# Adaptive-norm modulation of two feed-forward stages: running sums on VectorE in place of matmuls on TensorE

## Chip, cores, metric

One Trainium2 chip; the kernel runs on one of its cores. The metric is the device time of one execution in microseconds. The engines are TensorE (PE; its weight loads are listed apart as PEld), VectorE (DVE), ScalarE (ACT), GpSimd (POOL) and SyncE (SP), whose queue issues the DMAs here.

## What is computed

Two layers of a hybrid backbone over 512 latent tokens and 256 context tokens, width 1024. Each layer is a half-step SwiGLU feed-forward, a mixer of four head groups, and a second half-step feed-forward. Each of the three parts is modulated by vectors that come from one conditioning vector per stream (`c` for the latent, `c_ctx` for the context tokens):

```
mod   = (silu(c)     @ w_mod[l] + b_mod[l]).reshape(BATCH, 9, 1, 1024)
mod_c = (silu(c_ctx) @ w_mod[l] + b_mod[l]).reshape(9, 1, 1024)
x  = x  + 0.5 * mod[:, 2] * swiglu(modulate(rms_norm(x,  norm_g[l, 0]), mod[:, 0], mod[:, 1]), ffn_w_in[l, 0], ffn_w_out[l, 0])
xc = xc + 0.5 * mod_c[2]  * swiglu(modulate(rms_norm(xc, norm_g[l, 0]), mod_c[0],  mod_c[1]),  ffn_w_in[l, 0], ffn_w_out[l, 0])
...
```

`w_mod[l]` is 1024 x 9216 in f32, 37.7 MB for each of two layers. It is read once, and only two vectors are multiplied by it. In the second layer the context stream needs no output, so the context's vectors 5 to 8 are not needed there.

## The kernel before

The feed-forwards run in the order (layer 0, i = 0), mixer, (0, 1), (1, 0), mixer, (1, 1); they are called the first to the fourth below. `ffn` splits the 2816 hidden columns into 22 steps of 128. For each step `up` (line 520 for its matmuls) makes seven products of 12 matmuls out of the loaded weights `w1r`: ScalarE takes the high part `w1h` (line 460), VectorE the low part `w1l` (line 461) and the sums and differences of weights (line 479), in four buffers each. VectorE then combines the products (lines 525, 568, 581, 586). After every chunk of 3 or 2 steps (`CK` is 3, 2, 2, 3, 3, 3, 3, 3) the down-projection follows: products `y` (lines 448, 450, 452) with `w2h` and `w2l`, which VectorE adds to the residual `xT` (line 615). In the program the products of a step are put in before the down-projection of the chunk ahead of it, so both interleave on TensorE.

Modulation runs in the background of the first three feed-forwards, in blocks of 512 columns: 14, 6 and 12 blocks, from the list `bg` in `build`. A block is loaded in two halves of 1 MB (`mod_load`, line 229, one buffer `wm`); per half `mod_some` issues four f32 matmuls (line 241). Each has the 32-column tile `sc` (the two vectors and zeros) as its weight and 512 columns of `w_mod` as moving data, and writes its own 32 rows of one PSUM bank. After the second half ScalarE copies the bank to `mrow` (line 210), four matmuls against `pick` (line 218) add up the four row groups and transpose them, and VectorE adds the result to `mod` (line 221).

What sets the order: the program is written with tiles, and the framework puts each engine's instructions into a fixed order when the program is built, by the order of issue in the program and by priorities. `high_priority(offset=-LATER)` with `LATER = 300` places what is inside it as if it had been issued 300 instructions later; `mod_load` and `mod_some` stand inside it. `mod_flush` is called at fixed places of `up` at normal priority. On the chip every engine, and SP's queue of DMA issues, takes its instructions strictly in that order. The last chunk of the second feed-forward reuses the buffers `pc`, `sg` and `wm` for nine held tiles (`held_open`).

Of the kernel before, what the change touches and what calls it, by code (L numbers as in the profile page):

```python
# [18 lines left out]
F32 = mybir.dt.float32  # L19
# [4 lines left out]
ALU = mybir.AluOpType  # L24
# [4 lines left out]
KT = 8  # L29
# [3 lines left out]
DEPTH = 2  # L33
DFF = 2816
# [37 lines left out]
def more_constants():  # L72
    f = np.float64
    r = np.arange(128)
    d = r % 64

    ax = np.zeros((128, 128)); sq = np.zeros((128, 128))
    for i in range(128):
        h = i % 32
        j = i + 16 if h < 16 else i - 16  # L80
        ax[j, i] = -1.0 if h < 16 else 1.0
        h = i % 64
        j = i + 32 if h < 32 else i - 32
        sq[j, i] = -1.0 if h < 32 else 1.0
    tok = np.arange(SEQ)
    inv16 = (1.0 / (np.float32(ROPE_BASE) ** (np.arange(0, 32, 2, dtype=np.float32) / np.float32(32)))).astype(np.float32)
    inv32 = (1.0 / (np.float32(ROPE_BASE) ** (np.arange(0, 64, 2, dtype=np.float32) / np.float32(64)))).astype(np.float32)
    pos = np.where(d[:, None] < 32, tok[None, :] // GRID_W, tok[None, :] % GRID_W).astype(np.float32)
    aa = (pos * inv16[d % 16][:, None]).astype(np.float32).astype(f)
    sa = (tok[None, :].astype(np.float32) * inv32[d % 32][:, None]).astype(np.float32).astype(f)  # L90

    lg = np.log1p(-np.exp2(-5.0 - np.arange(4)))
    i = np.arange(128)
    rel = i[None, :] - i[:, None]
    dm = np.zeros((128, 4, 2, 128))
    for h in range(4):
        dm[:, h, 0] = np.where(rel >= 0, np.exp(np.maximum(rel, 0) * lg[h]), 0) / 8
        dm[:, h, 1] = np.where(rel <= 0, np.exp(np.maximum(-rel, 0) * lg[h]), 0) / 8
    qs = np.zeros((128, 2, 2, 128)); ks = np.zeros((128, 2, 2, 2)); gc = np.zeros((128, 2))
    for j in range(2):  # L100
        for e in range(2):
            g = lg[2 * j + e]
            qs[64 * e:64 * e + 64, j, 0] = np.exp((i + 1) * g)[None, :]
            qs[64 * e:64 * e + 64, j, 1] = np.exp((128 - i) * g)[None, :]
            ks[:, j, 0, e] = np.exp((127 - i) * g) / 8
            ks[:, j, 1, e] = np.exp(i * g) / 8
            gc[64 * e:64 * e + 64, j] = np.exp(128 * g)
    mean64 = (r[:, None] // 64 == r[None, :] // 64) / 64.0
    comb = r[:, None] % 32 == np.arange(2)[None, :]

    mp = np.where(i[None, :] >= i[:, None], 0, NEG)
    mn = np.where(i[None, :] <= i[:, None], 0, NEG)
    c32 = lambda *xs: np.concatenate([x.reshape(128, -1) for x in xs], 1).astype(np.float32)
    return {"k_rope": c32(ax, sq, np.cos(aa), np.sin(aa), np.cos(sa), np.sin(sa), mean64),
            "k_ret": c32(dm, qs, ks, gc), "k_win": c32(mp, mn), "k_comb": c32(comb)}
# [6 lines left out]
class Whole:  # L122
# [90 lines left out]
    def mod_add(self, l, b, row):  # L213

        nc = self.nc
        pt = self.psum("modpt", "ms")
        for j in range(4):
            nc.tensor.matmul(pt[:, 2 * j:2 * j + 2], lhsT=row[:, j * 128:(j + 1) * 128], rhs=self.pick, start=True, stop=True)  # L218
        for v in range(2):
            m = self.mod[l][v][:, b:b + 4]  # L220
            nc.vector.tensor_tensor(out=m, in0=pt[:, v:8:2], in1=m, op=ALU.add)
# [25 lines left out]
    def mod_flush(self):  # L247
        if self.mod_row:
            self.mod_add(*self.mod_row)
            self.mod_row = None  # L250

    def scales(self, l, n, v):

# [294 lines left out]
    def ffn(self, l, i, segs, chunks, background, last_cb, switch):  # L548
        nc, a = self.nc, self.a
        w2 = a["ffn_w_out"]  # L550
        H = self.half
        self.mod_now = self.mod_row = None
        self.mod_todo = [(*t, h) for t in background for h in range(2)]
        f = 0
        for ci, cn in enumerate(chunks):
            gs = []
            for j in range(cn):
                ff = f + j
                first = l == i == ff == 0
                if ff == 0:  # L560
                    ahead = self.up(l, i, 0, first)
                    if first:
                        self.first_shifts()
                    else:
                        self.raw_rows(self.fw, segs)
                t, g, p = ahead
                n1 = 2 * H
                mul = lambda eng, out, x, y: eng.tensor_tensor(out=out, in0=x, in1=y, op=ALU.mult)  # L568
                mul(nc.vector, g[:, :H], p[:, 2:H + 2], self.rsb[:, :H])
                mul(nc.vector, g[:, H:], g[:, H:], self.rsb[:, H:])  # L570
                mul(nc.vector, t[:, 2:], t[:, 2:], self.rsb)
                if first:
                    b = self.bias0
                else:
                    b = self.fw.tile([128, 2, 2], F32, name="ub", tag="ub", bufs=2)
                    nc.scalar.copy(b[:, 0, :], t[:, 0:2])
                    nc.scalar.copy(b[:, 1, :], p[:, 0:2])
                for s, (o, n) in enumerate(segs):
                    nc.scalar.activation(out=g[:, o:o + n], in_=g[:, o:o + n], func=AF.Silu, bias=b[:, 1, s:s + 1])
                for s, (o, n) in enumerate(segs):  # L580
                    nc.vector.scalar_tensor_tensor(out=g[:, o:o + n], in0=t[:, 2 + o:2 + o + n], scalar=b[:, 0, s:s + 1], in1=g[:, o:o + n],
                                                   op0=ALU.add, op1=ALU.mult)
                gh = self.hl.tile([128, n1], F32R, name="gh", tag="gh", bufs=max(chunks))
                gl = self.hl.tile([128, n1], F32R, name="gl", tag="gl", bufs=max(chunks))
                nc.scalar.activation(out=gh[:, :n1], in_=g[:, :n1], func=AF.Copy)  # L585
                nc.vector.tensor_tensor(out=gl[:, :n1], in0=g[:, :n1], in1=gh[:, :n1], op=ALU.subtract)
                gs.append((gh, gl))
                with self.tc.high_priority(offset=-LATER):
                    if ff:
                        self.mod_some()  # L590
                    else:
                        self.mod_load()

                if ff < DFF // 128 - 1:
                    ahead = self.up(l, i, ff + 1, False)
                if j == cn - 2:
                    wo = self.raw.tile([128, cn, D], F32, name="wo", tag="wo", bufs=1)
                    for q in range(cn):
                        nc.sync.dma_start(out=wo[:, q, :], in_=w2[l, i, (f + q) * 128:(f + q + 1) * 128, :])
            self.mod_flush()  # L600
            if ci == 0:
                gt = self.gates(l, 2 * i, segs, 0.5)
            if ci == len(chunks) - 1:
                if switch:
                    switch()
                else:
                    self.held_open([(self.fw, "pc", NPC, 1), (self.fw, "sg", 1, 2), (self.raw, "wm", 1, 3)])
            for n_ in range(KT):
                wh, wl = self.split(wo[:, :, n_ * 128:(n_ + 1) * 128], [128, cn, 128], "w2")
                py = [self.psum("y", "u")[:, :n] for o, n in segs]  # L610
                for j in range(cn):
                    self.mm3(py, wh[:, j, :], wl[:, j, :], gs[j][0], gs[j][1], segs, j == 0, j == cn - 1)
                for s, (o, n) in enumerate(segs):
                    xs = self.xT[n_][:, o:o + n]
                    nc.vector.scalar_tensor_tensor(out=xs, in0=py[s], scalar=gt[s][:, n_:n_ + 1], in1=xs, op0=ALU.mult, op1=ALU.add)  # L615
                if ci == len(chunks) - 1:
                    if switch is None and last_cb == self.fin_tile:

                        if n_:
                            last_cb(n_ - 1)  # L620
                        if n_ == KT - 1:
                            last_cb(n_)
                    else:
                        last_cb(n_)
            f += cn
# [454 lines left out]
    def ffn_open(self, ctx):  # L1080
        self.raw = self.pool(ctx, "raw", 3)
        self.hl = self.pool(ctx, "hl", 2)
        self.fw = self.pool(ctx, "fw", 2)
        self.pick = self.fw.tile([128, 2], F32, name="pick", bufs=1)
        self.nc.sync.dma_start(out=self.pick, in_=self.a["k_comb"])

    def first_mods(self):

# [633 lines left out]
```

## Time and profile before

| | us |
|---|---|
| median of 3 runs | 3520.66 (3515.94 to 3521.97) |
| the profiled execution | 3524.8 |
| its span from first to last instruction | 3522.7 |

| engine | busy us | share of the span |
|---|---|---|
| TensorE matmul | 3323.0 | 94% |
| TensorE weight load | 2799.4 | 79% |
| VectorE | 2403.3 | 68% |
| ScalarE | 1536.0 | 44% |
| GpSimd | 163.6 | 5% |

Durations below come from the profiled execution. Busy time is the time in which at least one instruction of the engine runs; neighbouring instructions overlap a little, so the sum of durations can be larger. In the chain that ended last the products of the up-projection (line 520) hold 32% of the span, the `y` products 18%, the modulation's matmuls (line 241) 2% and their transposes (line 218) 1%.

### The profile page before, as it was taken

How to read it: one execution, taken by the hardware profiler on the slowest of the kernel's cores; microseconds unless marked ns; L12 is line 12 of the kernel's file. 1: busy time of each engine (PE TensorE's matmuls, PEld its weight loads, DVE VectorE, ACT ScalarE, POOL GpSimd, SP SyncE). 2: the span in 40 equal slices, each digit the busy share in tenths (PEclk: the TensorE clock that was granted, in tenths of full speed). 3: DMA queues.
4: the chain of work that ended last, by engine and by line, in shares of the span. 5: the costliest groups of instructions: out<-in, count | busy, mean ns of one | idle time of the engine just before them, and what ended most of it. 6: DMA issues, size and time to landing. Idle time of an engine off the chain costs nothing.

```text
span 3522.7 us, 58995 instructions
## 1 busy us (share of the span) xinstructions
PE 3323.0 (94%) x23204; PEld 2799.4 (79%) x23204; DVE 2403.3 (68%) x5252; ACT 1536.0 (44%) x3342; POOL 163.6 (5%) x342
## 2 busy tenths in 40 slices
PE   6999999999998997999999899999999989989998
PEld 3888889777775664998999788988788776658997
DVE  5667667555547776676677866666645567868887
ACT  4333333422447653443344533433433467644554
POOL 0000000000003220000000000000000012300000
PEclk8899999999999898999999899999999989999999
DMA  5333333211100002233321233333312100022332
GB/s 184 108 121 122 103 108 107 81 43 43 43 14 1 11 16 71 77 97 111 104 67 51 90 102 111 110 98 105 102 54 56 37 9 7 19 86 88 108 99 72
DMA packets 329861, 267.63 MB, mean 76 GB/s; under 512 B 30676, under 2 KB 278640, under 8 KB 329584
## 3 DMA queue, kind: packets, MB, share of 16 engines
q1 hardware_dynamic: 329584, 263.87, 24.1%
q8 instruction: 182, 2.98, 0.3%
q14 instruction: 95, 0.78, 0.1%
HBM read 261.72 MB, written 2.10 MB: 75 GB/s over the span
## 4 chain that ended last, share of the span: by engine, by line
PE 81%; DVE 12%; ACT 4%; DMA 2%; issue 1%; POOL 1%; SPq 0%; DVEq 0%; ACTq 0%; POOLq 0%
PE ul L520 32%; PE y L448 6%; PE y L452 6%; PE y L450 6%; PE pj L448 4%; PE pj L450 4%; PE pj L452 4%; PE op L1479 3%; PE modps L241 2%; PE S L1224 1%; PE ch L959 1%; PE modpt L218 1%; DVE xtmp L902 1%; PE po L1224 1%; PE gram L830 1%
## 5 line engine op out<-in xcount | busy, mean ns | idle before, releaser
L520 PE MATMUL ul<-bh,w1h 128*128 128x386 f32 (+3 forms) x2464 | 809.2, 329 | 17.0 <-ACT w1h L460 6.1
L520 PE MATMUL ul<-bl,w1h 128*128 128x386 f32 (+3 forms) x2464 | 804.6, 327 | 0.6 <-DVE bl L348 0.4
L520 PE MATMUL ul<-bh,w1l 128*128 128x386 f32 (+3 forms) x2464 | 801.8, 326 | 2.7 <-DVE w1l L461 2.6
L460 ACT ACTIVATE w1h<-w1r 128x512 fp32r<-128x512 f32 x528 | 328.8, 631 | 491.4 <-PE ul L520 441.0
L520 PEld LDWEIGHTS ul<-bh,w1h 128*128 128x128 f32 x2464 | 467.9, 190 | 50.5 <-issue 20.1
L461 DVE TENSOR_TENSOR w1l<-w1r,w1h 128x512 fp32r<-128x512 f32 x528 | 360.3, 689 | 193.1 <-ACT w1h L460 185.4
L520 PEld LDWEIGHTS ul<-bl,w1h 128*128 128x128 f32 x2464 | 469.0, 190 | 9.5 <-issue 4.2
L520 PEld LDWEIGHTS ul<-bh,w1l 128*128 128x128 f32 x2464 | 467.3, 190 | 6.7 <-DVE w1l L461 4.2
L615 DVE SCALAR_TENSOR_TENSOR xT<-y,gate,xT 128x512 f32<-128x512 f32 x448 | 267.3, 631 | 176.5 <-PE y L452 174.3
L448 PE MATMUL y<-gh,w2h 128*128 128x512 f32 x1232 | 350.5, 351 | 8.5 <-ACT gh L585 8.3
L452 PE MATMUL y<-gh,w2l 128*128 128x512 f32 (+1 forms) x1232 | 346.3, 349 | 6.9 <-DVE w2l L461 6.8
L450 PE MATMUL y<-gl,w2h 128*128 128x512 f32 (+1 forms) x1232 | 348.4, 348 | 0.0
L460 ACT ACTIVATE w2h<-wo 128x384 fp32r<-128x384 f32 (+1 forms) x256 | 124.9, 496 | 345.3 <-PE y L450 299.7
L448 PE MATMUL pj<-hh,pwh 128*128 128x512 f32 (+2 forms) x864 | 251.7, 342 | 3.3 <-DVE qA L1151 1.8
L452 PE MATMUL pj<-hh,pwl 128*128 128x512 f32 (+2 forms) x864 | 242.8, 336 | 1.5 <-DVE pwl L461 1.5
L450 PE MATMUL pj<-hl,pwh 128*128 128x512 f32 (+2 forms) x864 | 242.8, 336 | 0.0
L448 PEld LDWEIGHTS y<-gh,w2h 128*128 128x128 f32 x1232 | 199.8, 190 | 49.9 <-ACT gh L585 13.5
L452 PEld LDWEIGHTS y<-gh,w2l 128*128 128x128 f32 x1232 | 198.1, 190 | 45.1 <-DVE w2l L461 11.3
L450 PEld LDWEIGHTS y<-gl,w2h 128*128 128x128 f32 x1232 | 199.0, 190 | 36.8 <-DVE u L568 5.9
L448 PEld LDWEIGHTS pj<-hh,pwh 128*128 128x128 f32 x864 | 146.6, 190 | 29.0 <-issue 7.9
L452 PEld LDWEIGHTS pj<-hh,pwl 128*128 128x128 f32 x864 | 143.4, 190 | 19.5 <-issue 5.1
L450 PEld LDWEIGHTS pj<-hl,pwh 128*128 128x128 f32 x864 | 143.8, 190 | 17.6 <-issue 7.6
(376 smaller groups left out, 5081.9 us busy)
## 6 DMA issues: line engine op xcount, KB each, us to landing
w1r<-in_ffn_w_in_dram SPq DMA_DIRECT2D x352, 256.0 KB
wm<-in_w_mod_dram SPq DMA_DIRECT2D x64, 1024.0 KB
wo<-in_ffn_w_out_dram SPq DMA_DIRECT2D x88, 512.0 KB
pw<-in_w_in_dram SPq DMA_DIRECT2D x46, 512.0 KB
wm<-in_w_mod_dram SPq DMA_DIRECT2D x32, 256.0 KB
pw<-in_w_in_dram SPq DMA_DIRECT2D x16, 256.0 KB
wo<-in_w_out_dram SPq DMA_DIRECT2D x128, 32.0 KB
wo<-in_w_out_dram SPq DMA_DIRECT2D x64, 64.0 KB
```

What stands on the lines that cost most here:

```text
L218: nc.tensor.matmul(pt[:, 2 * j:2 * j + 2], lhsT=row[:, j * 128:(j + 1) * 128], rhs=self.pick, start=True, stop=True)
L241: nc.tensor.matmul(self.mod_ps[32 * k:32 * k + 32, :], lhsT=self.sc[:, 4 * h + k, :], rhs=self.mod_w[:, k, :], start=h == 0, stop=h == 1, ...
L448: nc.tensor.matmul(p, lhsT=wh, rhs=xh[:, o:o + n], start=first, stop=False)
L450: nc.tensor.matmul(p, lhsT=wh, rhs=xl[:, o:o + n], start=False, stop=False)
L452: nc.tensor.matmul(p, lhsT=wl, rhs=xh[:, o:o + n], start=False, stop=last)
L460: nc.scalar.activation(out=hi, in_=raw, func=AF.Copy)
L461: nc.vector.tensor_tensor(out=lo, in0=raw, in1=hi, op=ALU.subtract)
L520: nc.tensor.matmul(out, lhsT=w[:, m, :], rhs=x[:, m, x0:], start=start and m == j == 0, stop=m == KT // 2 - 1 and j == 2, skip_group_check ...
L615: nc.vector.scalar_tensor_tensor(out=xs, in0=py[s], scalar=gt[s][:, n_:n_ + 1], in1=xs, op0=ALU.mult, op1=ALU.add)
L830: nc.tensor.matmul(pt[:, c, w], lhsT=BK[:, c, :], rhs=AR[:, e, c, w], start=True, stop=True)
L1224: mm = lambda out, lt, r, st, sp: nc.tensor.matmul(out, lhsT=lt, rhs=r, start=st, stop=sp, skip_group_check=True)
L1479: nc.tensor.matmul(p, lhsT=wt[:, i, :], rhs=os[i][:, osegs[i][v][0]:osegs[i][v][0] + c], start=i == 0, stop=i == m - 1)
```

## The change

In the second and third feed-forward a block of modulation is no longer multiplied on TensorE. `mod_block` loads the eight 128-row pieces of the block one by one (256 KB each, two buffers `wm` of 128x512). For each vector it lets VectorE multiply the first piece by that vector's 128 values, one for each partition, and add the other seven to a running sum `macc0` or `macc1`. One step later `mod_sum` adds up the partitions: a matmul with `ones1` (its first column ones, the other 31 zero) as weight for each vector and half of the block, in four row groups of one bank; then ScalarE's copy, now 256 columns, two matmuls against four new columns of `pick`, and VectorE's addition to `mod`. For layer 1 and columns from 40 x 128 on, only the latent vector is summed. Blocks start at evenly spaced steps: 0, 3, 7, 10, 14, 17 for 6 blocks and 0, 1, 3, 5, 7, 8, 10, 12, 14, 15, 17, 19 for 12. `mod_block` stands inside `high_priority(offset=-LATER)`, `mod_sum` does not. The first feed-forward keeps `mod_load`, `mod_some` and `mod_flush`.

```diff
-    comb = r[:, None] % 32 == np.arange(2)[None, :]
+    comb = np.concatenate([r[:, None] % 32 == np.arange(2)[None, :], r[:, None] == 32 * np.arange(4)[None, :]], 1)
...
+    def mod_block(self, l, b):
+        nc = self.nc
+        vs = range(2) if l < DEPTH - 1 or b < 40 else range(1)
+        acc = [self.fw.tile([128, 512], F32, name=f"macc{v}", tag=f"macc{v}", bufs=1) for v in vs]
+        for k in range(KT):
+            r = self.raw.tile([128, 512], F32, name="wm", tag="wm", bufs=2)
+            nc.sync.dma_start(out=r, in_=self.a["w_mod"][l, k * 128:(k + 1) * 128, b * 128:b * 128 + 512])
+            for v in vs:
+                s = self.sc[:, k, v:v + 1]
+                if k == 0:
+                    nc.vector.tensor_scalar(out=acc[v], in0=r, scalar1=s, scalar2=None, op0=ALU.mult)
+                else:
+                    nc.vector.scalar_tensor_tensor(out=acc[v], in0=r, scalar=s, in1=acc[v], op0=ALU.mult, op1=ALU.add)
+        self.macc = l, b, vs, acc
+
+    def mod_sum(self):
...
+        pt = self.psum("modps", "ms")
+        for v in vs:
+            for h in range(2):
+                g = 2 * v + h
+                with self.tc.high_priority(offset=g):
+                    nc.tensor.matmul(pt[32 * g:32 * g + 32, :256], lhsT=self.ones1, rhs=acc[v][:, 256 * h:256 * h + 256], start=True, stop=True)
+        m = 64 * len(vs)
+        row = self.work.tile([128, 256], F32, name="mrow", tag="t3")
+        nc.scalar.copy(row[:m], pt[:m, :256])
+        pt = self.psum("modpt", "ms")
+        for q in range(2):
+            nc.tensor.matmul(pt[:, 4 * q:4 * q + 4], lhsT=row[:m, q * 128:(q + 1) * 128], rhs=self.pick[:m, 2:], start=True, stop=True)
+        for v in vs:
+            m = self.mod[l][v][:, b:b + 4].rearrange("p (h q) -> p q h", q=2)
+            nc.vector.tensor_tensor(out=m, in0=pt[:, :8].rearrange("p (q v h) -> p q v h", q=2, v=2)[:, :, v, :], in1=m, op=ALU.add)
...
-        self.mod_now = self.mod_row = None
-        self.mod_todo = [(*t, h) for t in background for h in range(2)]
+        self.mod_now = self.mod_row = self.macc = None
+        self.mod_todo = [(*t, h) for t in background for h in range(2)] if l + i == 0 else []
+        at = {(q * (DFF // 128 - 1)) // len(background): t for q, t in enumerate(background)} if l + i else {}
...
                 gs.append((gh, gl))
+                self.mod_sum()
                 with self.tc.high_priority(offset=-LATER):
-                    if ff:
+                    if l + i:
+                        if ff in at:
+                            self.mod_block(*at[ff])
+                    elif ff:
                         self.mod_some()
                     else:
                         self.mod_load()
...
-                    self.held_open([(self.fw, "pc", NPC, 1), (self.fw, "sg", 1, 2), (self.raw, "wm", 1, 3)])
+                    self.held_open([(self.fw, "pc", NPC, 1), (self.fw, "sg", 1, 2), (self.raw, "wm", 2, 1), (self.fw, "macc0", 1, 1)])
...
-        self.pick = self.fw.tile([128, 2], F32, name="pick", bufs=1)
+        self.pick = self.fw.tile([128, 6], F32, name="pick", bufs=1)
         self.nc.sync.dma_start(out=self.pick, in_=self.a["k_comb"])
+        self.ones1 = self.fw.tile([128, 32], F32, name="ones1", bufs=1)
+        self.nc.gpsimd.memset(self.ones1, 0.0)
+        self.nc.gpsimd.memset(self.ones1[:, 0:1], 1.0)
```

## Rows read from the trace of the kernel before

**Rows 1.** Page: busy us, share of the span, instructions of each engine.
```profile
PE 3323.0 (94%) x23204; PEld 2799.4 (79%) x23204; DVE 2403.3 (68%) x5252; ACT 1536.0 (44%) x3342; POOL 163.6 (5%) x342
```

**Rows 2.** Main loops by stretch: us, busy PE, PEld, DVE, ACT, POOL; clock, DMA, GB/s.
```profile
1407.95:1920.85 512.90, 510.70 (x2916) 475.39 (x2916) 366.62 (x635) 199.80 (x395) 0.00 (x0) 1.00 0.28 87
1970.35:2520.40 550.05, 540.20 (x3071) 486.30 (x3071) 370.36 (x643) 204.71 (x403) 0.29 (x1) 1.00 0.33 105
```

**Rows 3.** The same view of line 241, then 218, second and third feed-forward.
```profile
1403.00:1960.00 557.00, 15.73 (x96) 2.19 (x96) 0.99 0.26 83
1966.00:2545.00 579.00, 31.80 (x192) 4.56 (x192) 0.99 0.34 107
...
1403.00:1960.00 557.00, 6.23 (x48) 5.81 (x48) 0.99 0.26 83
1966.00:2545.00 579.00, 12.51 (x96) 11.62 (x96) 0.99 0.34 107
```

**Rows 4.** Waits of TensorE for the copy, both stages: us in total, times, longest.
```profile
PE modpt L218 <- ACT mrow L210: 2.2, 3, 0.8
...
PE modpt L218 <- ACT mrow L210: 6.4, 9, 0.7
```

**Rows 5.** Instructions in order: start us, us, engine, line; in brackets the idle before.
```profile
2094.42 0.16 PEld L241 LDWEIGHTS modps<-wm,sc 128*32 128x32 f32 x8 [0.26 <-issue]
2094.42 1.06 PE L241 MATMUL modps<-wm,sc 128*32 128x512 f32 x8
...
2095.55 0.59 ACT L210 COPY mrow<-modps 128x512 f32<-128x512 f32 x1 [1.57 <-PE modps L241]
...
2096.19 0.97 PEld L218 LDWEIGHTS modpt<-pick,mrow 128*128 128x128 f32 x8 [1.61 <-ACT mrow L210]
2096.19 1.05 PE L218 MATMUL modpt<-pick,mrow 128*128 128x2 f32 x8 [0.71 <-ACT mrow L210]
...
2097.11 0.48 PE L448 MATMUL y<-gh,w2h 128*128 128x512 f32 x1
```

**Rows 6.** Groups by shape, a ScalarE copy of 256 columns: busy us, mean ns.
```profile
L535 ACT COPY pc<-ul 128x256 f32<-128x256 f32 x22 | 8.0, 362 | 4.4 <-PE ul L520 4.4
```

**Rows 7.** The same view of VectorE: multiply-add and multiplication by a scalar.
```profile
L581 DVE SCALAR_TENSOR_TENSOR sg<-u,ub,sg 128x512 f32<-128x512 f32 x87 | 64.9, 746 | 8.0 <-ACT sg L579 7.4
...
L581 DVE SCALAR_TENSOR_TENSOR sg<-u,ub,sg 128x256 f32<-128x256 f32 x65 | 31.1, 478 | 0.0
L1247 DVE TENSOR_SCALAR P<-P,st 128x512 f32<-128x512 f32 x16 | 7.8, 485 | 0.4
```

**Rows 8.** VectorE in order of time: a pair of multiply-adds and the next instruction.
```profile
1442.88 1.14 DVE L581 SCALAR_TENSOR_TENSOR sg<-u,ub,sg 128x512 f32<-128x512 f32 x2
1443.94 0.68 DVE L461 TENSOR_TENSOR w1l<-w1r,w1h 128x512 fp32r<-128x512 f32 x1
```

**Rows 9.** By stretch, columns of rows 2: up-projection, then the chunk's down-projection.
```profile
1425.00:1470.00 45.00, 45.00 (x259) 44.73 (x258) 37.38 (x59) 24.70 (x47) 0.00 (x0) 1.00 0.24 71
1470.00:1493.00 23.00, 23.00 (x133) 19.32 (x132) 11.55 (x21) 5.08 (x10) 0.00 (x0) 1.00 0.17 58
```

**Rows 10.** The same view: about the first seven steps of the third feed-forward.
```profile
1970.35:2146.00 175.65, 173.28 (x977) 157.60 (x978) 120.54 (x208) 68.00 (x135) 0.00 (x0) 0.99 0.35 111
```

**Rows 11.** Waits of TensorE for VectorE's low parts, second feed-forward.
```profile
PE y L452 <- DVE w2l L461: 4.1, 3, 2.5
```

**Rows 12.** Chain that ended last, pieces that are loads: start us, us.
```profile
64.71 2.69 DMA w1r<-in_ffn_w_in_dram
...
159.61 6.40 DMA wm<-in_w_mod_dram
...
1382.83 4.85 DMA w1r<-in_ffn_w_in_dram
```

**Rows 13.** Waits of VectorE, second feed-forward: us in total, times, longest.
```profile
DVE xT L615 <- PE y L452: 62.6, 49, 2.7
...
DVE w1s L479 <- DMA w1r<-in_ffn_w_in_dram: 0.9, 1, 0.9
```

More of the change, by code (lines that the diff above doesn't have):

```diff
@@ L217, in mod_add @@
         for j in range(4):
-            nc.tensor.matmul(pt[:, 2 * j:2 * j + 2], lhsT=row[:, j * 128:(j + 1) * 128], rhs=self.pick, start=True, stop=True)
+            nc.tensor.matmul(pt[:, 2 * j:2 * j + 2], lhsT=row[:, j * 128:(j + 1) * 128], rhs=self.pick[:, 0:2], start=True, stop=True)
         for v in range(2):
@@ L250, in mod_flush @@
             self.mod_row = None
+    def mod_block(self, l, b):
[13 more added lines that the diff above has]
+    def mod_sum(self):
+        if self.macc is None:
+            return
+        nc = self.nc
+        l, b, vs, acc = self.macc
+        self.macc = None
+        pt = self.psum("modps", "ms")
[13 more added lines that the diff above has]
+            nc.vector.tensor_tensor(out=m, in0=pt[:, :8].rearrange("p (q v h) -> p q v h", q=2, v=2)[:, :, v, :], in1=m, op=ALU.add)
     def scales(self, l, n, v):
```

## The prediction

> **What bounds the kernel now.** I read the totals of the page first, then the same engines cut to the two stages that the change touches, and only then single lines. The totals [rows 1] say that TensorE is busy for 94% of the span and VectorE for 68%. An average over stages proves little, so the table by stretch is the view that counts [rows 2]. Its first row is the second feed-forward (layer 0, i = 1) from its first product to the last one of its main loop, its second row the third feed-forward (layer 1, i = 0), up to the last `y` products. The granted clock is 1.00 in both. In the first, TensorE is busy 510.70 of 512.90 us and VectorE 366.62; in the second 540.20 of 550.05 and 370.36. So in both stages TensorE sets the end, VectorE has 146 us and 180 us to spare, and whatever leaves TensorE's queue shortens the stage, as long as VectorE stays off the path.
>
> **What the change removes from TensorE.** The second feed-forward carries 6 blocks of 512 modulation columns, the third 12. Each block is now 8 f32 matmuls of 512 columns, written as two groups of four (line 241), one copy of the sum by ScalarE (line 210) and 4 transposing matmuls (line 218). The time in which TensorE runs line 241 is 15.73 + 31.80 us in the two stages, and line 218 takes 6.23 + 12.51 us [rows 3]. TensorE also stands still for the ScalarE copy 3 + 9 times, 2.2 + 6.4 us [rows 4]. A stretch of the third feed-forward shows the shape of it: the group of four runs 1.06 us, the copy 0.59 us, a gap of 0.71 us, the transposes 1.05 us, and the next `y` products stand behind it, not beside it [rows 5]. Sum removed: 15.73 + 31.80 + 6.23 + 12.51 + 2.2 + 6.4 = 74.9 us, about 4.2 us a block.
>
> One caution on the 50 us to come, from the same rows: in the 1.06 us of a group the weight loads take only 0.16 us [rows 5]. Were TensorE held up by its loads alone, the group would have cost it little; but the `y` products behind it start only after the whole 1.06 us. Perfetto Trace Analysis, "Identifying the Most-Contended Engine", in the Trainium skill, holds that the busy share of matmuls is a poor measure and that weight loading shows how loaded TensorE is. By that rule the change would be worth what rival 4 says; the rows speak against it here.
>
> **What it adds to TensorE.** `mod_sum` folds the partitions with two or four f32 matmuls of 256 columns in one group. No row has that shape; half of the 512-column group is 0.53 us, which I take as the nearest, between the 0.16 us of the loads alone and the 1.06 us of a whole group [rows 5]. The transposes are 2 in place of 4: half of (6.23 + 12.51)/18, so 0.52 us. The copy is now 256 columns wide, 362 ns [rows 6] against 0.59 us [rows 5], so the gap of 0.71 us becomes 0.49 us; I keep it for 12 of 18 blocks as now. Sum: 18 x (0.53 + 0.52) + 12 x 0.49 = 24.8 us. TensorE's net saving is 74.9 - 24.8 = 50 us, with 41 and 57 as its bounds.
>
> **What it adds to VectorE.** A block costs 8 instructions for each of two vectors, and for one alone in the 8 blocks of layer 1 from column 40 on. That is 10 x 2 + 8 = 28 rows of 8: 28 multiplications by a scalar and 196 multiply-adds, all 128x512 f32. The same two forms are in the trace at 485 ns and 746 ns [rows 7]. A 512- and a 256-wide multiply-add in a row (746 + 478 ns) are followed by the next instruction after 1.06 us [rows 8], so neighbours overlap by some 0.08 us and I take 0.66 us. 28 x 0.485 + 196 x 0.66 = 143 us; 160 us without that overlap. Of it 12/28 = 61 us falls on the second feed-forward and 82 us on the third. The load becomes (366.6 + 61)/(512.9 - 16) = 86% and (370.4 + 82)/(550 - 34) = 88%. On average there is room, and the question is where. In a stretch of up-projection VectorE is busy 37.38 of 45 us (three steps), in the down-projection behind it 11.55 of 23 us [rows 9]. So 7.6 + 11.4 = 19 us are free for each chunk of three steps, and a block of two vectors needs 14 x 0.66 + 2 x 0.485 = 10.2 us. The instructions are put in with a priority lowered by 300, so they should fall into these holes.
>
> The crowded place is the beginning of the third feed-forward, where blocks start at steps 0, 1, 3 and 5. There VectorE is busy 120.54 of 175.65 us [rows 10]. Four blocks make it 120.54 + 4 x 10.2 = 161 us, and the stretch shrinks by 4 x (4.2 - 1.5) to about 165 us: 98%. I charge 5 us there (0 to 20).
>
> **The new waits.** (a) TensorE is served in order, and `mod_sum` comes at normal priority behind running sums of low priority. Behind its first matmul stand the products of the next step. Nothing in the trace waits this way; the nearest rows are TensorE's waits for VectorE's `w2l`, 3 times, 4.1 us, longest 2.5 us [rows 11]. Below nothing is excluded, since the term counts waiting alone. I take 0.7 us a block, what it waits for the copy today: 12.6 us (0 to 18 x 2.5 = 45). (b) VectorE is served in order too, and each of 144 loads of 256 KB now has a running sum waiting for it, with only two buffers. Behind that sum stand `w1l`, `w2l` and the evacuations, and behind them TensorE. The load goes out through SP's one queue, where it waits for the sum two before it, with `w1r` and `wo` loads behind it. Where the chain of waits runs over such loads, it waits 2.69 to 4.85 us for the ones of 256 KB and 6.40 us for one of 1 MB [rows 12]. Cover is the four `w1h`/`w1l` buffers, three products of 45/21 = 2.1 us [rows 9] ahead of TensorE, and VectorE waits for `w1r` only 0.9 us today [rows 13], so SP's queue runs well ahead. I take 6 us for both stages (0 to the 72 us of rival 3). Bytes moved stay the same, at a third of the DMA engines' time [rows 2].
>
> Edits with one answer: `pick` gets 4 more columns, `ones1` is two memsets on an engine with 5% load [rows 1], the first feed-forward keeps its way, and the tiles held for the last chunk stay nine. Nothing for these; if the memsets, eight in all, lay on the path, each would cost no more than the 0.49 us of a 512-wide scalar instruction [rows 7], 4 us together.
>
> **Sum.** -50 + 5 + 12.6 + 6 = -26 us against the profiled execution, 3524.8 us (span 3522.7 us and 2.1 us around it): 3498.8 us. The median of the runs shown, 3520.66 us, lies 4.1 us below that execution, so I predict 3495 us.
>
> **Rivals.**
> 1. All of it: the low-priority sums are always done when `mod_sum` comes up, and no load is late. -50 us: 3471 us. For it: the spare time of [rows 2], and that of the 12.1 us in which TensorE idles there the copies of [rows 4] make up 8.6, so that little else stalls it today. Against it: VectorE's load near 87% in a fixed order.
> 2. The wait moves: TensorE reaches `mod_sum` before the sums are complete and stands there. At 50/18 = 2.8 us a block, just over the longest wait of [rows 11], nothing is left: 3517 to 3521 us. For it: the sums have the low priority and the matmul that needs them the normal one. Against it: in the third stage a block has 550/12 = 46 us for its sums of 10.2 us or half of that.
> 3. Slower: a running sum at VectorE's head waits for its load and holds up `w1l` until TensorE runs out of weights. If each of the 144 loads costs TensorE 0.5 us, a quarter of the spread between the two 256-KB loads of [rows 12], that is 72 - 50 = +22 us: 3543 us. It decides from 50/144 = 0.35 us a load. For it: two buffers, one queue, landings of 2.7 us and more. Against it: the cover of three products, and that VectorE waits 62.6 us for `y` in the second feed-forward alone [rows 13], time in which a late load costs nothing.
> 4. The change takes out TensorE time that other work hid: if only weight loads count, a block's loads fall from 2 x 0.16 + 0.97 us [rows 5] to half of that, 0.16 + 0.49 us, and 18 blocks give 18 x 0.64 = 11.5 us: 3509 us. For it: the loading share of 88 to 93% in [rows 2] leaves a little air. Against it: the order of starts in [rows 5]. It is what the page named above would make of this change.
>
> **How the numbers follow.** My forecast (3480 to 3510 us) has 0.50, rival 1 0.18, rival 2 0.12, rival 3 0.17, rival 4 0.03. Differences under 0.2% (7 us) cannot be told from no change here. Faster gets the forecast, rivals 1 and 4 and a little of rival 2: 0.72. Same gets most of rival 2: 0.11. Slower 0.17. The range for 8 in 10 leaves out the far part of rival 3 and the last few us of rival 1: 3468 to 3532 us.
>
> **What would show it.** TensorE's two stages shorter by some 10 and 16 us. Line 241 gone there, and sum and transposes near 1.05 us a block. About 0.66 us from one running sum to the next, VectorE near 86 to 88%. TensorE's wait at the sum's matmul near 0.7 us. Wrong would be: VectorE's idle time ended by `w_mod` loads with TensorE waiting for `w1l` (rival 3), or waits of 2 us and more in front of the sum's matmuls (rival 2).

## The result and the profile after

The changed kernel takes 3473.47 us (median of 4 runs, 3472.36 to 3474.53) against 3521.31 us for the kernel before on the same chip (3515.94 to 3530.31): a ratio of 0.9862, 95% interval 0.9841 to 0.9882, 48 us less. A second series gave 3466.93 against 3525.2 us, 0.9833 (0.9817 to 0.985). The forecast was 3495 us, so the sign was right and the gain about twice the 26 us of the sum; the size is that of rival 1, "all of it", 3471 us, which had a chance of 0.18. The range for 8 in 10, 3468 to 3532 us, holds the result near its lower end.

The profiled execution has a span of 3472.0 us (3474.53 us with what lies around it). The totals of its page, in the columns of [rows 1]:

```profile
PE 3283.7 (95%) x22956; PEld 2791.2 (80%) x22956; DVE 2526.4 (73%) x5468; ACT 1531.6 (44%) x3342; POOL 163.8 (5%) x350
```

TensorE has 39 us less to do, VectorE 123 us more. The same main loops as in [rows 2], then each whole stage, from its first sum of squares to the next stage's (us, busy PE, PEld, DVE, ACT, POOL; clock, DMA, GB/s):

```profile
1399.87:1898.00 498.13, 498.13 (x2842) 471.62 (x2843) 419.84 (x732) 198.87 (x395) 0.22 (x2) 1.00 0.30 91
1946.50:2475.00 528.50, 522.55 (x2944) 486.56 (x2944) 449.24 (x786) 207.37 (x413) 0.29 (x1) 0.99 0.38 113
1395.43:1943.79 548.36, 529.81 (x3000) 498.02 (x3000) 463.85 (x817) 231.83 (x464) 0.22 (x2) 0.98 0.28 85
1943.79:2500.81 557.02, 550.03 (x3091) 510.33 (x3091) 471.56 (x830) 221.31 (x437) 1.42 (x3) 0.99 0.37 111
```

The whole stages of the kernel before, second and third:

```profile
1403.07:1965.36 562.29, 541.62 (x3073) 500.11 (x3073) 410.67 (x721) 232.63 (x464) 0.00 (x0) 0.98 0.26 82
1965.36:2557.18 591.82, 577.45 (x3267) 517.35 (x3268) 402.40 (x710) 224.41 (x437) 1.42 (x3) 0.99 0.33 105
```

The second feed-forward is 13.9 us shorter, the third 34.8 us, 48.7 us together: the whole difference of the medians lies in the two stages that were edited. VectorE stands at 419.84/498.13 = 84% and 449.24/528.50 = 85% there, and TensorE still sets the end.

What the change put into the stages, as groups by line (busy us, mean ns, then idle time before them and what ended most of it); they answer to [rows 3] and [rows 7]:

```profile
L265 DVE SCALAR_TENSOR_TENSOR macc<-wm,sc,macc 128x512 f32<-128x512 f32 x196 | 144.0, 747 | 8.6 <-DMA wm<-in_w_mod_dram 8.2
L263 DVE TENSOR_SCALAR macc<-wm,sc 128x512 f32<-128x512 f32 x28 | 13.4, 481 | 0.4 <-DMA wm<-in_w_mod_dram 0.4
L280 PE MATMUL modps<-macc,ones 128*32 128x256 f32 x112 | 14.5, 390 | 2.2 <-DVE macc L265 2.1
L286 PE MATMUL modpt<-pick,mrow 128*128 128x4 f32 (+1 forms) x72 | 10.1, 245 | 0.0
```

The last number of the third line is what the forecast's wait (a) came to: TensorE stood 2.1 us in all at the sums. TensorE's waits in the third feed-forward (us in total, times, longest) put it beside the others, to be read against [rows 4] and [rows 11]:

```profile
PE ssps L335 <- DVE ss L309: 14.1, 1, 14.1
PE y L491 <- DVE w2l L500: 3.0, 1, 3.0
PE modps L280 <- DVE macc L265: 2.1, 3, 1.3
PE ul L559 <- ACT pc L567: 0.6, 1, 0.6
```

The 14.1 us are the way into this stage: they end where its length, as measured here, begins. The wait for the ScalarE copy, 6.4 us in [rows 4], is gone, and in the second feed-forward neither it nor a wait for a sum appears at all.

How a block of two vectors ends in the second feed-forward, in order of time (start us, us; idle before in brackets; answers to [rows 5]):

```profile
1438.01 0.74 DVE L265 SCALAR_TENSOR_TENSOR macc<-wm,sc,macc 128x512 f32<-128x512 f32 x1
...
1439.27 0.63 PE L280 MATMUL modps<-macc,ones 128*32 128x256 f32 x4
...
1441.00 0.75 DVE L265 SCALAR_TENSOR_TENSOR macc<-wm,sc,macc 128x512 f32<-128x512 f32 x1
...
1442.15 0.63 PE L280 MATMUL modps<-macc,ones 128*32 128x256 f32 x4
...
1442.82 0.37 ACT L283 COPY mrow<-modps 128x256 f32<-128x256 f32 x1 [0.64 <-PE modps L280]
...
1443.34 0.52 PE L286 MATMUL modpt<-pick,mrow 128*128 128x4 f32 x4
```

The first vector's sum is folded at 1439.27 us, the second's 2.9 us later, when its last running sum is through, and between them, as between copy and transposes, `ul` products run. Nothing waits: the instructions of the block stand in TensorE's order where their operands are ready.

### The profile page after: what moved, and what is told of

It reads as the page before. It is cut to its first block, busy times and chain, and to the rows that moved or that the text cites. A ratio compares the mean times of both kernels' runs of the same rounds, so it can differ in the third digit from the quotient of the medians.

```text
span 3472.0 us, 58882 instructions
## 1 busy us (share of the span) xinstructions
PE 3283.7 (95%) x22956; PEld 2791.2 (80%) x22956; DVE 2526.4 (73%) x5468; ACT 1531.6 (44%) x3342; POOL 163.8 (5%) x350
## 4 chain that ended last, share of the span: by engine, by line
PE 80%; DVE 12%; ACT 4%; DMA 2%; issue 1%; POOL 1%; SPq 0%; DVEq 0%; ACTq 0%; POOLq 0%
PE ul L559 32%; PE y L487 6%; PE y L491 6%; PE y L489 6%; PE pj L487 4%; PE pj L489 4%; PE pj L491 4%; PE op L1527 3%; PE S L1272 1%; DMA wm<-in_w_mod_dram 1%; PE ch L1004 1%; PE modps L241 1%; DVE xtmp L947 1%; PE gram L875 1%; PE po L1272 1%
```

## The experiments

Stage lengths by the profiles, measured as above; "rest" is what comes after the third feed-forward, "mixer" what lies between the first and the second:

```
                        first  mixer  second  third  both    rest   median of the run
before                  685.2  717.9  562.3   591.8  1154.1  965.5  3521.31
changed                 681.6  713.8  548.4   557.0  1105.4  971.2  3473.47
changed, again          682.0  711.0  548.3   554.4  1102.7  964.2  3466.93
second only             683.9  711.0  548.3   594.6  1142.9  969.2  3508.74
third only              681.1  712.9  563.5   556.0  1119.5  973.8  3488.52
no modulation           680.9  723.0  539.1   532.4  1071.5  964.9  3441.17
loads, no running sums  682.4  716.4  549.8   549.1  1098.9  972.5  3471.32
running sums twice      680.8  713.0  553.0   596.2  1149.2  969.0  3514.69
one buffer              687.2  724.2  565.2   547.6  1112.8  966.7  3490.6
normal priority         682.3  713.2  550.2   564.7  1114.9  964.1  3476.18
evenly spread work      683.7  712.1  548.8   554.0  1102.8  970.8  3471.35
first stage too         657.2  711.9  548.6   554.1  1102.7  975.3  3444.12
first too, spread       657.1  715.1  547.6   554.8  1102.4  967.7  3444.43
```

Where a stage's code is the same, its length agrees within 3 us in most runs; "mixer" and "rest" swing by more although no experiment edits them, for the reason at the end. So I read the edited stages by themselves.

**The second stage alone.** The new way is used in the second feed-forward only.

```diff
-self.mod_todo = [...] if l + i == 0 else []
-at = {...} if l + i else {}
+self.mod_todo = [...] if (l, i) != (0, 1) else []
+at = {...} if (l, i) == (0, 1) else {}
```

> Only the second feed-forward (6 blocks) uses running sums; the third keeps its matmuls on TensorE. Theory 'covered' (VectorE's sums cost TensorE nothing, the gain is TensorE's own time): TensorE gives up 15.7 + 6.2 + 2.2 us there and gets back 4.5 + 3.2 us, so about -16 us against the kernel before, 3505 us. Rival 'elsewhere' (the gain lies outside the two stages, for the two profiles already differ by 7.6 us before the second feed-forward begins): -23 us or more for this half alone.

Measured: ratio 0.9963 (0.9947 to 0.998), and 14.0 us less in the second stage, the third 2.8 us longer. The medians differ by 14.0 us as well, so the gain lies in the stage and not elsewhere.

**The third stage alone.** The same edit with `(l, i) == (1, 0)`, and the held tiles of the last chunk of the second as in the kernel before.

> Only the third feed-forward (12 blocks) uses running sums; the second keeps its matmuls. Theory 'covered': TensorE gives up 31.8 + 12.5 + 6.4 us and gets back 10.0 + 6.9 us, about -34 us, 3487 us. Rival 'crowded' (VectorE at 98% in the first seven steps costs TensorE 5 to 20 us): -15 to -29 us. The two halves should add up to the whole -48 us if they are independent.

Measured: 0.9905 (0.9883 to 0.9926), 35.8 us less in the third stage, the second 1.2 us longer. That is above the 29 us at which the rival "crowded" ends. The two halves, 14.0 and 35.8 us, make up the 48.7 us of the whole within the agreement of the stages. Per block that is 14.0/6 = 2.3 and 35.8/12 = 3.0 us, on both sides of the 50/18 = 2.8 us that TensorE's own balance gives.

**No modulation in either stage.** This leaves out the blocks of both stages with their loads, so it shows the most that any way of computing them could gain.

```diff
-at = {...} if l + i else {}
+at = {}
```

> Leaves out the background modulation of the second and third feed-forward altogether: no loads of w_mod there, no sums, no matmuls, so the second layer runs with wrong modulation vectors. It gives the price of all that the change still pays. Theory 'covered': what remains in the changed kernel is TensorE's 14.5 us of sums and 10.1 us of transposes, so 25 us below the changed kernel, 3448 us. Rival 'hidden stalls' (VectorE or the loads still hold TensorE up): 35 us or more below it.

Measured: 3441.17 us, 0.9777 (0.9748 to 0.9805). The two stages take 1071.5 us against 1102.7 to 1105.4 us in the two profiles of the changed kernel, so what is left of the modulation costs 31 to 34 us. TensorE's own new work is 24.6 us of it, from these rows (line 280, then line 286, by stage of the changed kernel):

```profile
1395.43:1943.79 548.36, 4.45 (x48) 1.07 (x48) 0.98 0.28 85
1943.79:2500.81 557.02, 10.01 (x64) 2.36 (x64) 0.99 0.37 111
...
1395.43:1943.79 548.36, 3.21 (x24) 3.13 (x24) 0.98 0.28 85
1943.79:2500.81 557.02, 6.87 (x48) 6.36 (x48) 0.99 0.37 111
```

What remains for all stalls together is 7 to 9 us, 1.6 us of it in the second stage (548.4 - 539.1 - 7.7) and 5 to 8 us in the third (554.4 to 557.0, less 532.4 and 16.9). That lies between the two theories, of which one had none of it and the other 10 us or more. The forecast had charged 23.6 us.

The kernel before stands no better against this run. Its two stages are 1154.1 - 1071.5 = 82.6 us longer, its modulation takes TensorE 74.9 us with the waits for the copies [rows 3, 4], and 7.7 us are left over: 8.7 us in the third stage (59.4 - 50.7) and about nothing in the second (23.2 - 24.2). Stalls of this size were there already, and for both stages together the change moves them by less than 2 us.

**Loads without running sums.** The 196 multiply-adds are left out; loads, first multiplications, folding and transposes stay.

```diff
-                else:
-                    nc.vector.scalar_tensor_tensor(out=acc[v], in0=r, scalar=s, in1=acc[v], ...)
```

> The changed kernel with every load and every TensorE instruction, but of the 224 VectorE instructions only the 28 multiplications of the first pieces are left: the 196 multiply-adds (129 us of VectorE) are left out, so the second layer's vectors are wrong. Theory 'covered': within 4 us of the changed kernel, 3470 to 3477 us. Rival 'VectorE on the path': 10 us or more faster, because 129 us of work leave a path.

Measured: 3471.32 us, 0.9855 (0.9836 to 0.9875), 2 us from the changed kernel. The stages:

```profile
1398.76:1948.51 549.75, 530.18 (x3000) 498.14 (x3001) 418.13 (x733) 231.94 (x464) 0.22 (x2) 0.98 0.28 83
1948.51:2497.65 549.14, 545.95 (x3090) 508.35 (x3091) 411.77 (x718) 222.55 (x437) 1.42 (x3) 0.99 0.38 113
```

In the second stage 45.7 us of VectorE's time (463.85 - 418.13) cost nothing. In the third 59.8 us (471.56 - 411.77) cost 5 to 8 us, of which 2.5 us are the matmuls of four more folding groups (10.01 us on line 280 against 7.56 us here). And of the stalls that the run without modulation showed for this stage, 2.2 us (549.1 - 532.4 - 7.56 - 6.99) are there without any multiply-add. So the running sums are hidden in the first case and nearly so in the other.

**Running sums twice.** Each multiply-add is issued two times, so that VectorE has 196 more of them; the values are then other ones.

```diff
+                    for _ in range(2):
                         nc.vector.scalar_tensor_tensor(out=acc[v], in0=r, scalar=s, in1=acc[v], ...)
```

> The changed kernel with every one of the 196 multiply-adds issued twice (so the sums are wrong): 129 us more of VectorE, nothing more anywhere else. VectorE's load becomes (420 + 55)/498 = 95% in the second feed-forward and (449 + 74)/528 = 99% in the third. Theory 'covered up to the brim' (VectorE costs TensorE time only where its load comes near 100%, as in the first 300 us of the third feed-forward): second stage up by less than 10 us, third stage by 20 to 50 us, 3490 to 3530 us. Rival 'low priority always gives way' (the running sums never hold up anything): within 5 us of the changed kernel, 3470 to 3479 us.

Measured: 3514.69 us, 0.9974 (0.9962 to 0.9985): nearly the whole gain is lost. The third stage:

```profile
1946.80:2543.00 596.20, 567.04 (x3090) 520.20 (x3091) 542.35 (x942) 220.53 (x437) 1.42 (x3) 0.96 0.35 104
```

and the waits of TensorE in it (line numbers one higher by the edit):

```profile
PE ssps L336 <- DVE ss L310: 14.1, 1, 14.1
PE y L488 <- DVE xT L661: 13.1, 5, 7.8
PE ul L560 <- DVE w1l L501: 5.4, 3, 2.6
PE y L492 <- DVE w2l L501: 3.4, 2, 3.0
PE ul L560 <- ACT w1h L500: 3.3, 3, 1.1
PE modps L281 <- DVE macc L266: 2.7, 3, 2.0
```

The second stage bears the doubling for 4.6 us, the third pays 39 to 42 us. VectorE is busy for 91% of it, and TensorE now waits for evacuations (`xT`) and low parts (`w1l`, `w2l`), with the clock down to 0.96. It idles for 29.2 us of the stage instead of 7.0, and its busy time is 17 us longer. The loss has a place: set product by product beside the kernel without modulation, and less its own matmuls of modulation, this run is 40.6 us behind 248 us into the stage and 43.5 us at the end of the up-projection. From 1968 to 2195 us VectorE is busy for 93% and TensorE for 202.25 of 227 us, at a granted clock of 0.92; from 2195 to 2500 us VectorE is busy for 92%, and TensorE for 304.10 of 305 us, at 1.00. Even in this stage the wait at the sums' own matmuls is 2.7 us: what is lost when VectorE runs short is its other work, not the chain that was added.

**One buffer for the loads.** `wm` gets one buffer in place of two, and one more tile is held at the last chunk to keep the space as it was.

```diff
-            r = self.raw.tile([128, 512], F32, name="wm", tag="wm", bufs=2)
+            r = self.raw.tile([128, 512], F32, name="wm", tag="wm", bufs=1)
```

> The changed kernel with one buffer instead of two for the 256-KB pieces of w_mod, so each load waits for the running sums before it and each running sum for its own load, 144 times some 3 us one after the other. Theory 'covered' (VectorE's wait for a load falls into time that it does not need): within 5 us of the changed kernel, 3470 to 3479 us. Rival 'late loads hold up w1l': 0.1 to 0.5 us for each of the 144 loads, 15 to 70 us slower, 3488 to 3545 us.

Measured: 3490.6 us (3479.34 to 3496.36), 0.9905 (0.9883 to 0.9928). Part of the 17 us is the mixer, 724.2 us in this profile. The two stages are 7 to 10 us longer together, the second +17 and the third -7 to -9. The waits over both stages, of TensorE and then of VectorE:

```profile
PE ul L559 <- ACT w1h L499: 12.3, 1, 12.3
PE y L491 <- DVE w2l L500: 7.1, 4, 3.0
...
DVE macc L265 <- DMA wm<-in_w_mod_dram: 35.4, 42, 2.0
```

VectorE's waits for the loads grow from 8.6 to 35.4 us. The one wait of 12.3 us is at the boundary of the stages, where the first product of the third was written ahead of its sum of squares; that comes with a different order of the instructions, not with a late load. The median lies in the range of the rival, but TensorE's waits for `w1l`, by which the rival was to act, are 0.6 us in both stages. This run does not settle what one buffer costs by itself. It does show that 27 us more of VectorE waiting for loads cost TensorE 10 us at most.

**Normal priority.** The running sums are no longer put behind the other work.

```diff
-                with self.tc.high_priority(offset=-LATER):
+                with self.tc.high_priority(offset=0 if l + i else -LATER):
```

> The changed kernel with mod_block at normal priority in the second and third feed-forward, so that its sums stand in front of the weights' low parts of the next step and do not fill holes. Theory 'holes' (the low priority is what lets the sums lie where VectorE is free): a block's 10.2 us in one piece is more than the three products of lead, 6.4 us, so some 2 to 4 us a block of two vectors and less for one, 15 to 40 us slower, 3488 to 3513 us. Rival 'room enough' (at 85% load the order does not matter): within 5 us, 3470 to 3479 us.

Measured: 3476.18 us, 0.9872 (0.9856 to 0.9887), the second stage +1.8, the third +8 to +10 us. The median lies in the range of "room enough", the stages do not: I had expected 15 us and more, and the lowered priority, on which the forecast relied to bring the sums into VectorE's holes, is worth 10 to 12 us in the stages.

**Work evenly spread.** The blocks of the second and third stage are started by the work in them: blocks with two vectors and with one alternate, instead of four double blocks at the beginning of the third.

```diff
-at = {(q * (DFF // 128 - 1)) // len(background): t for q, t in enumerate(background)} if l + i else {}
+at = {}      # third: {0: 24, 2: 40, 3: 44, 5: 28, 7: 48, 9: 52, 10: 32, 13: 56, 14: 60, ...}
```

> The changed kernel with the 12 blocks of the third feed-forward in another order: blocks of two vectors and of one alternate, and their starts are spaced by VectorE work instead of by count, so that the first seven steps no longer hold four blocks of two vectors. Theory 'crowded' (the 8 us that the multiply-adds cost the third stage come from its first 300 us, where VectorE is 91% busy): 4 to 8 us faster than the changed kernel beside it, third stage 549 to 553 us. Rival 'spread anyway' (the loss does not depend on where the blocks lie): within 2 us of it.

Measured: 3471.35 us, 0.9844 (0.983 to 0.9857), on the same chip as the changed kernel again (3466.93). The third stage is 554.0 us against 554.4, and 557.0 in the first series: no gain of 4 to 8 us. So the 5 to 8 us of the third stage are not lost, for the most part, in its crowded beginning.

**The first feed-forward too.** All three stages use running sums (14 more blocks, all of two vectors), and one tile of two times 512 columns, which shares the space of `wm`, becomes two tiles.

```diff
-self.mod_todo = [...] if l + i == 0 else []
-at = {...} if l + i else {}
+self.mod_todo = []
+at = {...}
```

> The changed kernel with the first feed-forward's 14 blocks on VectorE too (28 more rows of 8, 143 us). TensorE would save 14 x 2.7 = 38 us there. VectorE was busy 384 us of that stage's 580 us, so it would be at 527 of 542 us, 97%. Theory 'covered up to the brim': the third stage lost 8 us to its sums at 91% over 300 us, so here a loss of 15 to 50 us against the 38 us: 3450 to 3485 us, likeliest near no change, 3470. Rival 'low priority always gives way': the full 38 us, 3436 us.

Measured: 3444.12 us (3438.28 to 3448.91), 0.9776 (0.9758 to 0.9795), faster than both kernels. The same stretch of the first feed-forward, here and then in the changed kernel:

```profile
105.00:600.00 495.00, 488.01 (x2774) 451.35 (x2775) 462.65 (x820) 184.78 (x374) 0.00 (x0) 0.99 0.41 121
...
105.00:600.00 495.00, 487.01 (x2797) 435.49 (x2796) 333.77 (x584) 182.34 (x358) 0.00 (x0) 1.00 0.35 112
```

The stage is 24.4 us shorter with VectorE at 93%. In TensorE's time it sheds 36.93 us of line 241, 13.65 us of line 218 and 5.6 us of copy waits, and takes up 15.49 + 7.48 us for the new matmuls: 33.2 us. So about 9 us are lost here against the matmuls, 4.0 us of it in waits for the sums (0.6) and for their copies (3.4). That is less than the 15 to 50 us that I had expected, and the run is 26 us faster than the 3470 us that I held likeliest.

**The first one too, spread as above.** Both edits together.

> All three feed-forwards on VectorE, with the third one's blocks in the even order. Theory 'crowded' and the 29 us of the run with all three on VectorE add up: 33 to 37 us below the changed kernel beside it, some 3438 to 3441 us. Rival 'spread anyway': 29 us below it, 3445 us.

Measured: 3444.43 us, 0.9766 (0.975 to 0.9782), the same as without the spreading.

**The changed kernel again**, unedited, for the spread of one kernel between runs:

> The changed kernel unaltered, as the yardstick for the two runs beside it, whose effects are a few us. Every theory expects 3474 us within 3 us, and a second and third stage of 548 and 557 us in the profile.

Measured: 3466.93 us (3462.01 to 3472.65), 6.5 us under the first series and outside the 3 us expected. Of the 12.1 us between the two profiled spans 2.7 us lie in the two edited stages, the rest in the others.

## Why the prediction was right in sign and half in size

**What bounds the kernel: right.** Time taken off TensorE's queue came off the stages, nearly one for one. TensorE's balance by the rows: 74.9 us removed [rows 3, 4], 24.6 us added, 2.1 us of waits at the sums, 48.2 us in all; the stages lost 48.7 us, and 51.4 us in the second profile of the changed kernel.

**What is removed, rival 4: refuted.** By TensorE's weight loads alone the change would have been worth 11.5 us, the value that I had drawn from "Identifying the Most-Contended Engine" in Perfetto Trace Analysis of the Trainium skill. That section names the share of weight loads, beside the share of peak arithmetic, as a measure of how far a kernel is from its roofline; to price one group of matmuls by it was my step. The change was worth 48 us. Over these f32 column tiles the time in which the engine runs the matmuls was the one that counted [rows 5].

**What TensorE takes over: right in sum, not in its parts.** The folding took 14.46 us instead of 9.5. Each group of 256 columns runs 0.63 us, not the 0.53 us of half a 512-column group, and there are 23 groups for 18 blocks, because in 5 of the 10 double blocks each vector is folded by itself, as in the timeline above. The transposes took 10.1 us (9.4 forecast), and the copy waits, 5.9 us forecast, are nil in both stages. 24.6 against 24.8 us: two errors that cancel.

**What VectorE takes over: too high, harmlessly.** 747 and 481 ns are the durations of [rows 7]. But VectorE's busy time in the stages differs from that without modulation by 463.85 - 411.60 = 52 us and 471.56 - 402.81 = 69 us, where 61 and 82 us were forecast; the rows without modulation are

```profile
1403.90:1943.03 539.13, 520.84 (x2928) 494.03 (x2928) 411.60 (x704) 231.15 (x458) 0.22 (x2) 0.98 0.21 64
1943.03:2475.41 532.38, 529.21 (x2979) 502.27 (x2979) 402.81 (x680) 220.37 (x425) 1.42 (x3) 0.99 0.23 69
```

An added multiply-add among other work therefore cost 0.54 us (52 us for 96 instructions, 69 us for 128), less than the 0.66 us from one start to the next.

**The crowded beginning: a charge for nothing new.** 5 us (0 to 20) were added to the time of the kernel before. The third stage does lose 5 to 8 us against the kernel without modulation, but on the same count the kernel before lost 8.7 us there, so the agreement with 5 us is luck and the change added nothing. The place was wrong too. Spreading the blocks did not bring the loss back, and set product by product beside the kernel without modulation, less its own matmuls of modulation, the changed kernel's third stage is 1.6 us behind after 192 us and 5.4 us after 515 us (0.7 and 3.9 us in the second profile): most of the loss comes behind the four double blocks. The trace shows one of its forms in the third stage:

```profile
2115.22 1.41 DVE L265 SCALAR_TENSOR_TENSOR macc<-wm,sc,macc 128x512 f32<-128x512 f32 x2 [0.99 <-DMA wm<-in_w_mod_dram]
...
2116.03 0.63 PE L280 MATMUL modps<-macc,ones 128*32 128x256 f32 x4 [0.46 <-DVE macc L265]
```

A load that is 0.99 us late becomes 0.46 us at TensorE. There are three waits at the sums, 2.1 us; the one of 1.3 us follows a load that VectorE waits 1.19 us for. Where the other 3 to 6 us go, no single row tells.

**Wait (a): the term that failed.** 12.6 us were taken, 0.7 us for each block, from what a block waited for its copy; 2.1 us came, in 3 of 18 blocks. The step treated the priority as if it set a distance between the last sum and the fold. What the trace shows is an order in which TensorE's fold stands behind the products that cover it. In 11 of the 18 blocks it starts 12 to 51 us after the last running sum; in the other 7 it starts within 1 us of it, in the timeline above 0.5 us for one vector and 0.4 us for the other, and the three waits are among these. A block has 44 us from its first multiplication to its last fold there (1398.3 to 1442.2 us), and 19 to 91 us in all 18, for sums of 5 or 10 us. The argument against rival 2 had that; I priced the term from waits of another kind in spite of it.

**Wait (b): failed too.** 6 us were charged and rival 3 had 72. VectorE does wait for the loads, 8.6 us in 17 places, or 0.06 us for each of the 144 instead of 0.35 us from which rival 3 decides, and TensorE waits for `w1l` no longer than before. Its cover is VectorE's idle time: it waits for `y` 31.0 us in the second stage, where [rows 13] had 62.6:

```profile
DVE xT L660 <- PE y L491: 31.0, 35, 1.6
...
DVE macc L265 <- DMA wm<-in_w_mod_dram: 1.3, 2, 1.1
```

Together the crowded beginning, (a) and (b) were 23.6 us of the forecast. The stalls that they stand for, all that is not the modulation's own time on TensorE, are 7.7 us in the kernel before and 7 to 9 us in the changed one. A forecast that adds to the time before has to count the difference, which is between -1 and +2 us. With that the same sum gives -50 us and a little less, and the stages lost 48.7 and 51.4 us.

**Was rival 1 the right account?** Its mechanism, sums always done and no load late, holds within 7 to 9 us, as the kernel without modulation shows, and its number, 50 us, within 2 us. Its condition, how far VectorE may be loaded, is what the runs add: 84% goes with a loss of 1.6 us, 85% with 5 to 8 us, 93% in the first feed-forward with some 9 us, counted there against the matmuls for want of a run without modulation, and the doubled sums with some 40 us more, nearly all in a stretch at 93% where TensorE waits for evacuations and low parts, while the 92% behind it cost about 3 us. So the load alone does not decide it. Which work of VectorE comes late counts beside it: those waits show it, and the run at normal priority, where the same work in another order costs the two stages 10 to 12 us, agrees.

## What to carry to other kernels

If a stage's trace shows one engine busy to 98% or more and another with a quarter of its time idle, count a move between them at the first engine's full balance, and price a new wait by the time that the producer has before its consumer comes up (here 19 to 91 us for sums of 5 or 10 us) and not by waits of another kind that the trace happens to show. Before you charge stalls to a change, count those that the kernel has already (here 7.7 us, by a run without the work). Find the limit by doubling the moved work: here the first load of it cost 7 to 9 us and a second one 44 to 47 more. If the kernel has a further stage of the same sort, move that too: here the first feed-forward gave another 24 us.

## What was not expected of the hardware

The length of stages with the same instructions in the same order goes with the granted clock. The mixer between the first and the second feed-forward, without modulation and in the changed kernel again:

```profile
680.90:1403.90 723.00, 667.34 (x5729) 498.77 (x5728) 447.85 (x1285) 333.82 (x803) 87.44 (x180) 0.95 0.11 30
...
682.00:1393.00 711.00, 652.76 (x5731) 486.25 (x5729) 447.04 (x1285) 333.70 (x803) 87.66 (x180) 0.98 0.11 31
```

The same matmuls are busy 14.6 us longer at a mean granted clock of 0.95 than at 0.98, and the stage takes 12 us more, a quarter of what the change is worth. In both, the first 360 us of the stage run at a granted clock of 1.00, the upper of its two levels; from 420 to 660 us into it, where TensorE is busy for 53 to 60 of each 60 us, the one has 0.97, 0.91, 0.83 and 0.98, the other 1.00 throughout. Why one execution gets the lower clock is open; no run here was made for it. In the second and third feed-forward, where TensorE hardly pauses, the clock is 0.98 or 0.99 by stage in all profiles but that of the doubled sums, whose third stage has 0.96.
